# Attention with eleven exponentials on VectorE: other groups, all passes on one engine, and a plan that counts dependent passes

## The chip, the cores and the metric

The kernel runs on one core of a Trainium2 chip. The metric is the device time of the program in microseconds; the median of the runs shown is compared. Engines work in parallel, each on its own queue in the order in which the program issues, and wait for each other by semaphores: TensorE (PE) multiplies, ScalarE (ACT) and VectorE (DVE) work element by element, GpSimd (POOL) does the same more slowly, SyncE (SP) issues DMAs.

## What is computed

Attention for 8 x 8 heads of 512 queries and 512 keys with 64 channels, in float32 at the borders:

```python
q, k, v: (8, 8, 512, 64) float32
scores = einsum('bhqd,bhkd->bhqk', q, k) / sqrt(64)
attn = exp(scores - scores.max(-1)); attn = attn / attn.sum(-1)
out = einsum('bhqk,bhkd->bhqd', attn, v)
```

The kernel leaves the maximum out (the quotient is the same) and takes the sum of a row from a column of ones beside v.

## The kernel before

**Tiling.** The 64 heads are taken as 32 pairs g. A pair's q, k and v come by three DMAs of 256 KB from SyncE's queue (`load`, L440) into buffers that hold seven pairs. Each is cast to float16 by GpSimd (`cast`, L446 and L456; 12 buffers of v, 5 of q with k). TensorE transposes q and k of a pair in eight steps (`transposes`, L480) into one PSUM bank, and VectorE copies them to SBUF (`copy`, L493). For a block of 128 keys by 512 queries one matmul makes the scores, keys on the partitions. Two blocks are a **group**: its scores `st` fill two PSUM banks, and there are three such buffers. Four groups belong to a pair, 129 "groups" in all, the last two being halves.

**Two ways to take the exponential.** Most groups go to ScalarE: one ACTIVATE over 128 x 1024 elements (L527) reads `st` and writes float16 `pt`. The groups in `ON_DVE`, eleven of them, go to VectorE. TensorE first puts a constant into `st` by two more matmuls (L508). VectorE's **raise** (L544) reads `st` from PSUM, scales it, cuts it off below and writes `z` to SBUF, which frees `st`. Three **passes** (L561) from SBUF to SBUF then work out a polynomial on the bits: y from z, y from y, and `pd` from y and z; each needs the one before. `z` and `y` have two buffers each, `pd` four.

The second pass of the last group of `ON_DVE` is an exception (`SHARED = 1`): GpSimd does it in two instructions (`middle`, L574 and L577).

**Values.** A unit of values is four matmuls (L604), blocks of `pt` or `pd` as weights against v with its column of ones, 65 columns out. Seven units share a PSUM bank `o`. When a bank is full, VectorE takes the reciprocal of the sums (L582) and multiplies (L584) into a ring of 56 units in SBUF (together a **norm**), and SyncE stores each head of four units (L593). Transposes and values take turns on the same two PSUM banks. The last head goes its own way: `last_values` (L620) and `finish` (L634, L635).

**What sets the order.** Engines take their instructions in the order in which the program issues them, and that order is made ahead by the class `Plan`. It steps through time by 5 ns with a table of durations (`EXP`, `COPY`, `NORM`, `RAISE`, `PASS` and so on) and decides what each engine does next. `step_pe` prefers scores when a buffer of `st` is free and ScalarE's backlog is short, and else takes transposes or values. `step_dve` takes, of what is ready, a copy that is needed soon, then a raise, then the oldest; passes only fill the time when nothing comes within the margins in `late`. `emit` writes a cast into the order beside a VectorE instruction that reads PSUM. The result is a list of steps that is issued as it stands. The plan's times are for ordering only; on the chip each instruction waits for its semaphores.

A cast can be tied to the VectorE instruction issued last before it (`cast_behind`, L467), by a semaphore, so that it doesn't run while a pass reads SBUF. The plan asks for this when its time is over `CALM`. A pair's v counts as late, and is loaded and cast 6 us later by the plan's due times, when its first group is in `ON_DVE`.

Of the kernel before, what the change touches and what calls it, by code (L numbers as in the profile page):

```python
# [8 lines left out]
FP32 = mybir.dt.float32  # L9
# [8 lines left out]
class Plan:  # L18
# [6 lines left out]
    COPY, NORM, RAISE = (601, 690), (307, 390), (1132, 1215)  # L25
    COPY_1 = (400, 190)
    NORM_COLUMN, PASS_DONE = 67, 80
    PASS, PASSES = 1131, 3
    OFFSET = 216
    FIRST_EXP = 5130  # L30
    STEP = 5
    CALM, KEEN = 14000, 6
    FIRST_UNIT = 4
    ON_DVE = (7, 20, 28, 40, 51, 56, 70, 80, 84, 98, 112)
    SHARED = 1

    LATE_NORM, LATE_COPY, HURRY, SOON, BACKLOG = 1000, 2200, 900, 80, 1200
    SLACK, AHEAD = 0, 2

    CAST, CAST_DONE, TO_POOL = 560, 130, 150  # L40
    MIDDLE, MIDDLE_DONE = (1000, 2250), 250
# [3 lines left out]
    def __init__(self, groups, pairs, first):  # L45
# [26 lines left out]

        late = {grp[0][0] for m, grp in enumerate(groups) if m in self.ON_DVE}
        due = []
# [79 lines left out]
    def for_dve(self, m):  # L154
        return m in self.ON_DVE

# [125 lines left out]
    def step_dve(self, t):  # L282
        if self.uncast and self.uncast[0][1:] == (1, "q"):
            if self.landed.get((1, "q"), 1e9) <= t:
                self.emit(t, None)
                self.dve = t + 240
                self.pool = self.port = t + 330
                self.cast_done[(1, "q")] = t + 400
            return
        now = [x for x in self.ready if x[0] <= t]  # L290
        if now:
            g = self.groups[min(self.m + 1, len(self.groups) - 1)][0][0]
            job = min(now, key=lambda x: (x[1] != "copy" or x[2][0] > g, x[1] != "raise", x[0]))
            self.ready.remove(job)
            _, kind, what = job
            slots = 2 if kind == "raise" else 1
            while slots and not self.casts and self.fits(t, 60 if slots == 1 else 0):
                self.emit(t, self.dve_done if self.dve_done > t - 300 else None)
                slots -= 1
                if slots and self.fits(t, 500):  # L300
                    self.emit(t, self.dve_done if self.dve_done > t - 300 else None)
                    slots -= 1
            self.note(t, kind, *what)
            if kind == "norm":
                more = self.NORM_COLUMN * what[1]
                self.dve = t + self.NORM[0] + more
                self.banks[what[2]] = t + self.NORM[1] + more + self.TO_PE
                for _ in range((what[0] + what[1]) // 4 - what[0] // 4):
                    self.loads.append(("store", self.dve + 100))
            elif kind == "finish":  # L310
                self.dve = t + self.NORM[0] + 2 * self.NORM_COLUMN
            elif kind == "copy":
                held, done = self.COPY if what[0] != 1 else self.COPY_1
                self.dve = t + held
                self.banks[what[1]] = self.tq[what[0]] = t + done + self.TO_PE
            else:
                self.dve = t + self.RAISE[0]
                self.read[what[0]] = t + self.RAISE[1] + self.TO_PE
                self.passes += [(what[0], s, 0) for s in range(self.PASSES)]
            self.dve_done = self.dve  # L320
        elif any(x[2] <= t for x in self.passes):
            m, s, _ = job = next(x for x in self.passes if x[2] <= t)
            end = max(t, self.port) + self.PASS
            late = {"copy": self.LATE_COPY, "norm": self.LATE_NORM, "raise": self.LATE_NORM, "finish": 0}
            if all(x[0] > end - late[x[1]] for x in self.ready):
                self.passes.remove(job)
                self.note(t, "pass", m, s)
                self.dve = self.port = self.dve_done = end
                if s == 0 and m in self.ON_DVE[len(self.ON_DVE) - self.SHARED :]:
                    self.passes.remove((m, 1, 0))  # L330
                    self.passes[self.passes.index((m, 2, 0))] = (m, 2, 1e9)
                    self.casts.append(("middle", m, end + self.TO_POOL))
                    self.note(end, "middle", m)
                if s == self.PASSES - 1:
                    self.exps[m] = end + self.PASS_DONE + self.TO_PE + self.SLACK

# [17 lines left out]
def kernel(  # L354
# [7 lines left out]
    nc = tc.nc  # L362
    B, H, S, D = q.shape
    P = 128
# [25 lines left out]
    opool = ctx.enter_context(tc.tile_pool(name="out", bufs=4))  # L390
# [17 lines left out]
    blocks = {}  # L408
    os = {}
    heads = []  # L410
    raised = {}
    first = {}
    last = {}

    def source(src, g):
        b, h = g // ppb, 2 * (g % ppb)
        return src[b, h : h + 2].rearrange("h (p i) d -> p h i d", i=NI)
# [12 lines left out]
    def load(g, names):  # L430
        if g >= NP:
            return
        for name in names:
            src = {"q": q, "k": k, "v": v}[name]
            t = load_tile(g, name)
            if name == "v" and g in HALVED:
                for h in range(2):
                    nc.sync.dma_start(out=t[:, h], in_=source(src, g)[:, h])
                continue
            nc.sync.dma_start(out=t[:, :, :, :], in_=source(src, g))  # L440
# [22 lines left out]
    def dve(ins):  # L463
        latest[:] = [ins]
        return ins
# [18 lines left out]
    def copy(g, n=0):  # L484
        if g == 1:
            dve(
                nc.vector.tensor_copy(
                    out=tqk[g][:, n], in_=tps[g][:, n].rearrange("p i c -> p (i c)")
                )
            )  # L490
            return
        dve(
            nc.vector.tensor_copy(  # L493
                out=tqk[g][:, :, :], in_=tps.pop(g).rearrange("p n i c -> p n (i c)")
            )
        )
# [74 lines left out]
    def middle(m):  # L571
# [4 lines left out]
        )  # L576
        nc.gpsimd.tensor_tensor(out=y[:, :, :], in0=t[:, :, :], in1=y[:, :, :], op=AluOp.mult)  # L577

    def normalise(u, n):
        o, x = os[u // 7], u % 7  # L580
        rc = opool.tile([P, 7, 1], FP32, tag="rc", name=f"rc_{u}")
        nc.vector.reciprocal(out=rc[:, 0:n], in_=o[:, x : x + n, D : D + 1])  # L582
        dve(
            nc.vector.tensor_tensor(  # L584
                out=ring[:, u % NU : u % NU + n, :],
                in0=o[:, x : x + n, 0:D],
                in1=rc[:, 0:n].broadcast_to([P, n, D]),
                op=AluOp.mult,
            )
        )  # L590
        while heads and heads[0][2] + NI <= u + n:
            g, h, u0 = heads.pop(0)
            nc.sync.dma_start(  # L593
                out=source(out, g)[:, h], in_=ring[:, u0 % NU : u0 % NU + NI, :]
            )
# [48 lines left out]
    def first_loads():  # L644
        tk = load_tile(0, "k")
        tq = load_tile(0, "q")
        for h in range(2):
            nc.scalar.dma_start(out=tk[:, h], in_=source(k, 0)[:, h])
            nc.sync.dma_start(out=tq[:, h], in_=source(q, 0)[:, h])
# [94 lines left out]
    with tc.manual_schedule():  # L744
        plan = Plan(groups, NP, 3)
        steps = plan.run()
        first_loads()
        for g, name in plan.first_loads:
            load(g, name)
        make_identity(nc, ident)  # L750
        nc.vector.memset(lift, LIFT[0])
        for p in (32, 96):
            nc.vector.memset(lift[p : p + 32], LIFT[1])
        for n in range(NV):
            nc.vector.memset(vps[n][:, :, :, D : D + 1], 1.0)
        first_pair()
        do = {
            "transposes": transposes,
            "scores": scores,
            "values": values,  # L760
            "load": load,
            "cast": cast_behind,
            "raise": raise_,
            "copy": lambda g, b: copy(g),
            "pass": pass_,
            "middle": middle,
            "last": last_values,
            "finish": finish,
            "norm": lambda u, n, b: normalise(u, n),
        }  # L770
        for what, *args in steps:
            do[what](*args)
# [30 lines left out]
```

## Time and profile before

| | |
|---|---|
| time, median of 3 runs | 117.99 us (117.93 to 118.18) |
| the profiled execution | 117.88 us, its span 116.1 us |
| granted TensorE clock, mean | 0.992 |
| first exponential starts | 5.11 us |
| last exponential ends | 112.74 us |
| ScalarE's exponentials L527 | 115, busy 104.8 us |
| VectorE's raises L544 and passes L561 | 11 and 32 |
| GpSimd's two instructions for one pass | 1.04 and 2.36 us |

The span is the time from the first to the last instruction of the profiled execution; the rest of its 117.88 us lies around it. Busy rows of one engine can overlap: an instruction's start is recorded before the end of the one ahead of it. So the pitch of an engine is read from start to start or from end to end, not from the durations. An idle time in brackets is the engine's, ahead of the first instruction of the row, with what ended it.

The tail, all engines in order of time (start us, duration us, engine, line):

```profile
111.54 1.21 ACT L527 ACTIVATE pt<-st 128x512 f16<-128x512 f32 x2
112.31 0.79 PE L620 MATMUL o_last<-vp,pt 128*128 128x65 f16 x12 [0.19 <-ACT pt L527]
113.14 0.17 DVE L634 RECIPROCAL rc_last<-o_last 128x2 f32<-128x2 f32 x1
113.34 0.29 DVE L635 TENSOR_TENSOR obl<-o_last,rc_last 128x128 f32<-128x128 f32 x1
113.66 0.35 ACTq L642 DMA_DIRECT2D out_dram<-obl  x1
```

The last values wait for the last exponential, two short VectorE steps follow, and the last store ends the program.

### The profile page before, as it was taken

Reading aid. Unit: us, or ns where it says so; the run is one execution under the profiler, and the core shown is the slowest. Engines: PE = TensorE matmul, PEld = TensorE weight load, DVE = VectorE, ACT = ScalarE, POOL = GpSimd, SP = SyncE. Lnnn points to the kernel's source line nnn. Section 1 sums busy time; section 2 is a strip of 40 time slices with the busy share of each in tenths; the row PEclk is TensorE's granted clock in tenths of the full one; section 3 lists DMA queues with packets and bytes.
Section 4 is the critical chain, followed back from the end, with each engine's and each line's share of the span. In section 5 each row is a group of like instructions: output and inputs, shape, how many; then the busy total and the mean of one; then the engine's idle time right before and its main releaser. Section 6 shows DMA issues by size and latency. Waiting matters only on the chain.

```text
span 116.1 us, 4085 instructions
## 1 busy us (share of the span) xinstructions
PE 104.8 (90%) x1581; PEld 66.9 (58%) x1581; DVE 101.4 (87%) x177; ACT 109.7 (95%) x122; POOL 60.5 (52%) x104
## 2 busy tenths in 40 slices
PE   7979989989999999999799979999989999999980
PEld 2635557546676466646465646467845567576660
DVE  3455997699999999999999999999999999969381
ACT  4599999999999999999999999999999999999980
POOL 2378519954653655555425546954484255596000
PEclk9999999999999999999999999999999999999996
DMA  3999999999999999999999999999999994222354
GB/s 109 286 372 380 384 378 384 388 375 375 344 323 319 307 293 336 311 338 307 352 307 305 321 328 241 296 376 324 329 292 358 366 291 167 93 93 93 101 184 133
DMA packets 35604, 33.83 MB, mean 291 GB/s; under 512 B 2688, under 2 KB 35584, under 8 KB 35584
## 3 DMA queue, kind: packets, MB, share of 16 engines
q1 hardware_dynamic: 35152, 33.24, 87.1%
q10 hardware_dynamic: 432, 0.33, 0.9%
q8 instruction: 12, 0.20, 0.7%
q14 instruction: 8, 0.07, 0.2%
HBM read 25.17 MB, written 8.39 MB: 289 GB/s over the span
## 4 chain that ended last, share of the span: by engine, by line
ACT 31%; DVE 30%; PE 18%; DMA 10%; issue 7%; POOL 1%; SPq 0%; POOLq 0%; ACTq 0%
ACT pt L527 29%; DVE y L561 7%; DVE tqk L493 6%; DMA k<-in_k_dram 6%; DVE z L544 6%; PE st L522 6%; PE o L604 6%; DVE ring L584 5%; DMA v<-in_v_dram 4%; DVE pd L561 4%; PE st_0a L653 3%; ACT pt L703 2%; PE tp L480 2%; POOL qkp L456 1%; DVE rc L582 1%
## 5 line engine op out<-in xcount | busy, mean ns | idle before, releaser
L527 ACT ACTIVATE pt<-st 128x1024 f16<-128x1024 f32 (+1 forms) x115 | 104.8, 1216 | 0.0
L522 PE MATMUL st<-tqk 64*128 64x512 f16 (+1 forms) x250 | 44.6, 380 | 4.3 <-ACT pt L527 3.1
L604 PE MATMUL o<-vp,pt 128*128 128x65 f16 x920 | 43.0, 194 | 1.4 <-DVE tqk L493 0.9
L604 PEld LDWEIGHTS <-pt 128*128 128x128 f16 x920 | 36.3, 98 | 11.0 <-issue 9.7
L446 POOL CAST vp<-v 128x512 f16<-128x512 f32 x32 | 19.6, 616 | 18.6 <-DVE y L561 10.9
L456 POOL CAST qkp<-k 128x512 f16<-128x512 f32 x31 | 19.0, 613 | 14.1 <-PE st L522 4.7
L584 DVE TENSOR_TENSOR ring<-o,rc 128x448 f32<-128x448 f32 (+2 forms) x37 | 22.6, 612 | 1.3
L456 POOL CAST qkp<-q 128x512 f16<-128x512 f32 x30 | 18.4, 613 | 10.1 <-DVE y L561 4.8
L522 PEld LDWEIGHTS <-tqk 64*128 64x128 f16 x250 | 13.1, 93 | 17.6 <-issue 10.1
L493 DVE COPY tqk<-tp 128x1024 f16<-128x1024 f16 x30 | 20.3, 683 | 2.3 <-PE tp L480 2.2
L480 PE MATMUL tp<-ident,qkp 128*128 128x128 f16 x248 | 20.5, 220 | 0.6 <-DVE tqk L493 0.2
L480 PEld LDWEIGHTS <-qkp 128*128 128x128 f16 x248 | 14.2, 97 | 8.8 <-issue 4.8
L561 DVE SCALAR_TENSOR_TENSOR pd<-y,z 128x1024 uint32<-128x1024 f32 x11 | 14.2, 1288 | 0.0
L544 DVE TENSOR_SCALAR z<-st 128x1024 f32<-128x1024 f32 x11 | 13.4, 1217 | 0.9 <-PE st L522 0.9
L561 DVE SCALAR_TENSOR_TENSOR y<-z 128x1024 f32<-128x1024 uint16 x11 | 13.9, 1261 | 0.1
L604 PE MATMUL o<-vp,pd 128*128 128x65 f16 x88 | 13.1, 194 | 0.3 <-DVE pd L561 0.2
L561 DVE SCALAR_TENSOR_TENSOR y<-y 128x1024 f32<-128x1024 f32 x10 | 12.3, 1234 | 0.0
L604 PEld LDWEIGHTS <-pd 128*128 128x128 f16 x88 | 8.6, 98 | 3.2 <-issue 2.4
L582 DVE RECIPROCAL rc<-o 128x7 f32<-128x7 f32 (+2 forms) x37 | 7.3, 196 | 3.3 <-PE o L604 3.2
L508 PE MATMUL st<-const-bfloat16-1.0,lift 64*128 64x512 bf16 x22 | 4.3, 381 | 0.4 <-ACT pt L527 0.4
L653 PE MATMUL st_0a<-const-bfloat16-1.0 128*128 128x512 bf16 (+1 forms) x11 | 3.5, 482 | 0.8 <-PEq L787 0.8
L653 PEld LDWEIGHTS <-const-bfloat16-1.0 128*128 128x128 bf16 x15 | 1.7, 129 | 2.5 <-issue 2.4
(50 smaller groups left out, 25.0 us busy)
## 6 DMA issues: line engine op xcount, KB each, us to landing
out_dram<-ring SPq DMA_DIRECT2D x63, 128.0 KB, 3.8
k<-in_k_dram SPq DMA_DIRECT2D x31, 256.0 KB, 5.1
q<-in_q_dram SPq DMA_DIRECT2D x31, 256.0 KB, 5.0
v<-in_v_dram SPq DMA_DIRECT2D x27, 256.0 KB, 5.2
v<-in_v_dram SPq DMA_DIRECT2D x10, 128.0 KB, 4.1
k<-in_k_dram ACTq DMA_DIRECT2D x2, 128.0 KB, 2.9
q<-in_q_dram SPq DMA_DIRECT2D x2, 128.0 KB, 2.7
out_dram<-obl SPq DMA_DIRECT2D x1, 64.0 KB, 1.6
```

The costliest lines, as they stand in the source:

```text
L446: return nc.gpsimd.tensor_copy(out=vps[g % NV][:, :, :, 0:D], in_=raw[g]["v"][:, :, :, :])
L456: return nc.gpsimd.tensor_copy(out=dst, in_=src[:, :, :, :])
L480: nc.tensor.transpose(tps[g][:, n, i, :], qkp[g][:, n, i, :], ident)
L493: nc.vector.tensor_copy(out=tqk[g][:, :, :], in_=tps.pop(g).rearrange("p n i c -> p n (i c)"))
L522: nc.tensor.matmul(st[:, x, cols], kc, qc[:, cols], start=not on_dve, stop=True)
L527: nc.scalar.activation(out=pt[:, :, cols], in_=st[:, :, cols], func=EXP, scale=scale)
L544: nc.vector.tensor_scalar(out=r["z"][:, :, :], in0=r["st"][:, :, :], scalar1=STEP, scalar2=2.0**17, op0=AluOp.mult, op1=AluOp.max,)
L561: nc.vector.scalar_tensor_tensor(out=r["bits"][:, :, :] if last else r["y"][:, :, :], in0=r["y"][:, :, :] if s else f, scalar=QUARTIC[s], ...
L582: nc.vector.reciprocal(out=rc[:, 0:n], in_=o[:, x : x + n, D : D + 1])
L584: nc.vector.tensor_tensor(out=ring[:, u % NU : u % NU + n, :], in0=o[:, x : x + n, 0:D], in1=rc[:, 0:n].broadcast_to([P, n, D]), op=AluOp. ...
L604: nc.tensor.matmul(os[u // 7][:, u % 7, :], blocks[(g, c, h)][:, y * P : (y + 1) * P], vps[g % NV][:, h, c, :], start=(c == 0), stop=(c == ...
L653: nc.tensor.matmul(dst[:, 0:n], ones[:, 0:P], ones[:, 0:n], start=True, stop=True)
```

## The change

- `ON_DVE` lists eleven other groups: 8, 20, 25, 41, 47, 56, 65, 78, 90, 100, 111 in place of 7, 20, 28, 40, 51, 56, 70, 80, 84, 98, 112. With it other pairs' v count as late, so the loads and casts change their order from the sixth load on.
- `SHARED = ()`: no pass goes to GpSimd.
- The plan lets a pass start only `CHAINED` (117 ns) after the end of the pass or raise it needs, so that other work can come between. Before, all three passes of a group were ready at once.
- `CALM` goes from 14000 to 20000, and the margins and thresholds of the plan change (`LATE_COPY`, `HURRY`, `BACKLOG`, `SLACK`, a new `LATE_MULT`).
- A reciprocal can be issued apart from its multiply (`recip` and `mult`, `invert`), if `APART` is set. It is `False`, and the order that is issued has no such step.

All the rest of the order follows from the plan.

```diff
--- before.py
+++ after.py
@@ -25,17 +25,19 @@
     COPY, NORM, RAISE = (601, 690), (307, 390), (1132, 1215)
     COPY_1 = (400, 190)
     NORM_COLUMN, PASS_DONE = 67, 80
+    RECIP, RECIP_DONE, CHAINED = 80, 230, 117
+    APART, ROOM = False, -200
     PASS, PASSES = 1131, 3
     OFFSET = 216
     FIRST_EXP = 5130
     STEP = 5
-    CALM, KEEN = 14000, 6
+    CALM, KEEN = 20000, 6
     FIRST_UNIT = 4
-    ON_DVE = (7, 20, 28, 40, 51, 56, 70, 80, 84, 98, 112)
-    SHARED = 1
-
-    LATE_NORM, LATE_COPY, HURRY, SOON, BACKLOG = 1000, 2200, 900, 80, 1200
-    SLACK, AHEAD = 0, 2
+    ON_DVE = (8, 20, 25, 41, 47, 56, 65, 78, 90, 100, 111)
+    SHARED = ()
+
+    LATE_NORM, LATE_MULT, LATE_COPY, HURRY, SOON, BACKLOG = 1000, 1600, 1800, 800, 80, 1800
+    SLACK, AHEAD = 100, 2
 
     CAST, CAST_DONE, TO_POOL = 560, 130, 150
     MIDDLE, MIDDLE_DONE = (1000, 2250), 250
@@ -293,6 +295,23 @@
             job = min(now, key=lambda x: (x[1] != "copy" or x[2][0] > g, x[1] != "raise", x[0]))
             self.ready.remove(job)
             _, kind, what = job
+            early = [x for x in now if x is not job and x[1] == "norm"] if self.APART else []
+            apart = kind == "norm" and self.APART and any(x[2] <= t for x in self.passes)
+            apart = apart and self.banks[1 - what[2]] <= t + self.ROOM
+            if kind == "norm" and (early or apart):
+                self.note(t, "recip", *what)
+                kind = "mult"
+                if not early:
+                    self.dve = t + self.RECIP
+                    self.ready.append((t + self.RECIP_DONE, "mult", what))
+                    return
+            for x in early:
+                self.ready.remove(x)
+                self.note(t, "recip", *x[2])
+                t += self.RECIP
+                self.ready.append((t + self.RECIP_DONE - self.RECIP, "mult", x[2]))
+            if early and kind == "mult" and job[1] == "norm":
+                t += self.RECIP_DONE - self.RECIP
             slots = 2 if kind == "raise" else 1
             while slots and not self.casts and self.fits(t, 60 if slots == 1 else 0):
                 self.emit(t, self.dve_done if self.dve_done > t - 300 else None)
@@ -301,8 +320,10 @@
                     self.emit(t, self.dve_done if self.dve_done > t - 300 else None)
                     slots -= 1
             self.note(t, kind, *what)
-            if kind == "norm":
+            if kind in ("norm", "mult"):
                 more = self.NORM_COLUMN * what[1]
+                if kind == "mult":
+                    more -= self.RECIP_DONE
                 self.dve = t + self.NORM[0] + more
                 self.banks[what[2]] = t + self.NORM[1] + more + self.TO_PE
                 for _ in range((what[0] + what[1]) // 4 - what[0] // 4):
@@ -316,21 +337,24 @@
             else:
                 self.dve = t + self.RAISE[0]
                 self.read[what[0]] = t + self.RAISE[1] + self.TO_PE
-                self.passes += [(what[0], s, 0) for s in range(self.PASSES)]
+                self.passes += [(what[0], s, 1e9 if s else self.dve + self.CHAINED) for s in range(self.PASSES)]
             self.dve_done = self.dve
         elif any(x[2] <= t for x in self.passes):
             m, s, _ = job = next(x for x in self.passes if x[2] <= t)
             end = max(t, self.port) + self.PASS
             late = {"copy": self.LATE_COPY, "norm": self.LATE_NORM, "raise": self.LATE_NORM, "finish": 0}
+            late["mult"] = self.LATE_MULT
             if all(x[0] > end - late[x[1]] for x in self.ready):
-                self.passes.remove(job)
                 self.note(t, "pass", m, s)
                 self.dve = self.port = self.dve_done = end
-                if s == 0 and m in self.ON_DVE[len(self.ON_DVE) - self.SHARED :]:
-                    self.passes.remove((m, 1, 0))
-                    self.passes[self.passes.index((m, 2, 0))] = (m, 2, 1e9)
+                after = self.passes.index(job)
+                del self.passes[after]
+                if s == 0 and m in self.SHARED:
+                    self.passes.remove((m, 1, 1e9))
                     self.casts.append(("middle", m, end + self.TO_POOL))
                     self.note(end, "middle", m)
+                elif s < self.PASSES - 1:
+                    self.passes[after] = (m, s + 1, end + self.CHAINED)
                 if s == self.PASSES - 1:
                     self.exps[m] = end + self.PASS_DONE + self.TO_PE + self.SLACK
 
@@ -408,6 +432,7 @@
     blocks = {}
     os = {}
     heads = []
+    rcs = {}
     raised = {}
     first = {}
     last = {}
@@ -576,10 +601,16 @@
         )
         nc.gpsimd.tensor_tensor(out=y[:, :, :], in0=t[:, :, :], in1=y[:, :, :], op=AluOp.mult)
 
+    def invert(u, n):
+        o, x = os[u // 7], u % 7
+        rcs[u] = opool.tile([P, 7, 1], FP32, tag="rc", name=f"rc_{u}")
+        dve(nc.vector.reciprocal(out=rcs[u][:, 0:n], in_=o[:, x : x + n, D : D + 1]))
+
     def normalise(u, n):
         o, x = os[u // 7], u % 7
-        rc = opool.tile([P, 7, 1], FP32, tag="rc", name=f"rc_{u}")
-        nc.vector.reciprocal(out=rc[:, 0:n], in_=o[:, x : x + n, D : D + 1])
+        if u not in rcs:
+            invert(u, n)
+        rc = rcs.pop(u)
         dve(
             nc.vector.tensor_tensor(
                 out=ring[:, u % NU : u % NU + n, :],
@@ -766,7 +797,9 @@
             "middle": middle,
             "last": last_values,
             "finish": finish,
+            "recip": lambda u, n, b: invert(u, n),
             "norm": lambda u, n, b: normalise(u, n),
+            "mult": lambda u, n, b: normalise(u, n),
         }
         for what, *args in steps:
             do[what](*args)
```

## The prediction

> **What bounds the kernel now.** I read the page's busy times first, then the busy time by stretch, then ScalarE's, VectorE's and GpSimd's instructions in order of time. The first two:
>
> ```profile
> span 116.1 us, 4085 instructions
> PE 104.8 (90%) x1581; PEld 66.9 (58%) x1581; DVE 101.4 (87%) x177; ACT 109.7 (95%) x122; POOL 60.5 (52%) x104
> ...
> core 0: us, PE busy (x) PEld busy (x) DVE busy (x) ACT busy (x) POOL busy (x), PEclk, DMA share, GB/s
> 5.00:21.00 16.00, 14.13 (x214) 8.90 (x212) 11.72 (x21) 15.89 (x19) 10.45 (x18) 1.00 1.08 379
> 21.00:41.00 20.00, 18.85 (x267) 11.68 (x265) 19.04 (x28) 20.00 (x23) 11.60 (x21) 1.00 1.03 346
> 41.00:61.00 20.00, 18.64 (x293) 12.03 (x290) 19.76 (x29) 19.96 (x23) 9.57 (x17) 1.00 1.00 319
> 61.00:81.00 20.00, 18.65 (x285) 11.88 (x285) 19.68 (x31) 20.00 (x23) 12.05 (x21) 1.00 0.99 312
> 81.00:101.00 20.00, 19.03 (x314) 12.55 (x313) 19.67 (x29) 20.00 (x23) 10.05 (x17) 1.00 0.85 280
> ```
>
> ScalarE is busy 20.00 of 20.00 us in three stretches; only 41 to 61 has a crack (19.96). VectorE is nearly as full from 21 to 101. Whether ScalarE loses anything shows in the ends of its exponentials (start plus duration; the starts overlap):
>
> ```profile
> 46.44 1.94 ACT L527 ACTIVATE pt<-st 128x1024 f16<-128x1024 f32 x2
> ...
> 47.34 1.95 ACT L527 ACTIVATE pt<-st 128x1024 f16<-128x1024 f32 x2
> ...
> 49.33 1.02 ACT L527 ACTIVATE pt<-st 128x1024 f16<-128x1024 f32 x1
> ...
> 49.33 1.94 ACT L527 ACTIVATE pt<-st 128x1024 f16<-128x1024 f32 x2
> ```
>
> The ends are 48.38, 49.29, 50.35, 51.27: steps of 0.91, 1.06, 0.92. Over the 112 steps between full exponentials, 110 are 0.915 to 0.918, one is 0.929 (46.5 us) and one 1.058 (50.3 us). So ScalarE waits 0.012 + 0.141 = 0.15 us in all, and the time is its work, 0.917 a group, plus the head and tail. The change leaves ScalarE's 115 exponentials, the head and the tail's last steps as they are. **The floor is therefore 117.88 - 0.15 = 117.73** on the profiled execution's own time (span 116.1 and 1.78 around it). The median of the runs, 117.99, is 0.11 above that execution.
>
> VectorE, from which ScalarE's waits come:
>
> ```profile
> 34.94 1.22 DVE L561 SCALAR_TENSOR_TENSOR y<-y 128x1024 f32<-128x1024 f32 x1
> 36.07 0.68 DVE L493 COPY tqk<-tp 128x1024 f16<-128x1024 f16 x1
> 36.67 0.20 DVE L582 RECIPROCAL rc<-o 128x7 f32<-128x7 f32 x1
> 36.90 0.62 DVE L584 TENSOR_TENSOR ring<-o,rc 128x448 f32<-128x448 f32 x1
> 37.44 1.51 DVE L561 SCALAR_TENSOR_TENSOR pd<-y,z 128x1024 uint32<-128x1024 f32 x1
> ...
> 48.28 1.22 DVE L544 TENSOR_SCALAR z<-st 128x1024 f32<-128x1024 f32 x1
> 49.53 1.23 DVE L561 SCALAR_TENSOR_TENSOR y<-z 128x1024 f32<-128x1024 uint16 x1
> ...
> 37.26 0.61 POOL L456 CAST qkp<-q 128x512 f16<-128x512 f32 x1
> 39.01 0.62 POOL L446 CAST vp<-v 128x512 f16<-128x512 f32 x1 [1.14 <-DVE pd L561]
> ```
>
> From start to start a pass or a raise costs 1.13, a copy 0.60, a reciprocal with its multiply 0.77. A pass straight behind its own input starts 1.25 later, not 1.13: 0.12 for the dependence. A pass that meets a cast is stretched: the one at 37.44 takes 1.51, 0.29 too long, while the cast of 37.26 runs to 37.87. Six passes are over 1.30 (1.35, 1.38, 1.51, 1.32, 1.60, 1.55), 1.4 us too much together.
>
> **Part by part.** *The shared group.* Group 112's second pass was two GpSimd instructions, 1.04 + 2.36 us; now all 33 passes are VectorE's. That is +1.13 on VectorE. Passes straight behind their own input fall from four to two in the order of the changed program: -2 x 0.12. Net +0.9 us. It lies in the tail: between 102.6 and 110 VectorE has waits for PE of 0.67, 0.26 and 1.62 us, 2.55 in all, and the last group is now 111. Cost 0; without that cover, 0.9.
>
> The Trainium skill (VectorE: DVE Perf Modes, The DRAIN you can't avoid) says that semaphores between chained VectorE operations cost nothing extra; by it the 0.12 would not exist and the net would be +1.13, still under the cover. The 1.25 beside 1.13 speaks against it here.
>
> *The new places.* VectorE has no idle time to speak of between 21.75 and 102.6, so I weigh its work from one raise to the next against ScalarE's groups between them. Before, 20 to 28: 1 raise, 3 copies, 2 norms, 2 passes = 1.13 + 1.80 + 1.54 + 2.26 = 6.74, against 7 x 0.917 = 6.42: +0.32. All ten so, before: -2.25, +0.32, -0.31, +0.24, -0.69, -0.25, +0.68, -0.42, -0.78, +0.53. After, with the counts of its order: -1.50, -0.03, -0.11, -0.78, +0.53, -0.60, -0.10, -0.03, -0.21, +0.07. The new load is evener. What a surplus does is seen in the trace: measured from raise 20 (21.75) at 0.917 a group, raises 28, 40, 51, 56, 70, 80, 84, 98, 112 start 0.47, 0.61, 0.86, 0.19, -0.03, 0.76, 0.34, -0.05, 0.49 late. ScalarE's two waits fall around the 0.86; 0.76 cost nothing. So I take the 0.15 as gone: -0.15 (bounds -0.15 and 0).
>
> *Around group 20.* In the new order TensorE issues the eight transposes of pair 6 ahead of the scores of 20, and VectorE their copy ahead of raise 20; before, both stood behind. Eight transposes hold PE about 0.55 (0.61 as a row with its drain), and the copy ends some 0.2 after the scores: raise 20 is 0.75 later. First, group 21's scores, next on PE, are later by as much. Before, they ended 0.33 ahead of the end of exponential 19, and waits begin when that lead falls under 0.2 (the 0.012 wait had 0.20). What PE does ahead of them also differs (six units of values of 0.13 where it had more), so the wait is between 0 and 0.23; I take the middle, 0.11. Second, the lateness goes on: 0.75 - 0.03 = 0.72 at raise 25, - 0.11 = 0.61 at raise 41, plus stretched passes: before, 0.59 came together from raise 20 to 51, of which I put 0.45 here: 1.06, which is 0.2 over the 0.86 that cost 0.15, so 0.35; with no stretch, 0. I take 0.15, nearer the low end, as a wait of ScalarE at 21 also takes off lateness. Queued behind a late raise on VectorE are the copy and norms, and for these PE waits, then the scores.
>
> *Casts without a wait.* The border from which a cast is tied to the last VectorE instruction moves from 14 to 20 us. In the new program five casts (v3, k5, q5, v2, v4) wait for their loads alone. Before, casts ran 0.68 apart as loads landed (8.18, 8.85, 9.53 up to 12.26), so these come at about 12.9 to 15.7, where group 8's passes run. The nearest row is the stretched pass, 0.11 to 0.38 each, so 0.3 to 1.15 for three. VectorE's cover is the idle time ahead of raise 20:
>
> ```profile
> 19.10 0.20 DVE L582 RECIPROCAL rc<-o 128x7 f32<-128x7 f32 x1 [0.33 <-PE o L604]
> ...
> 20.19 0.69 DVE L493 COPY tqk<-tp 128x1024 f16<-128x1024 f16 x1 [0.23 <-PE tp L480]
> 21.75 1.22 DVE L544 TENSOR_SCALAR z<-st 128x1024 f32<-128x1024 f32 x1 [0.87 <-PE st L522]
> ```
>
> These are 1.43 us, over 1.15: cost 0, bounds -0.1 (q5 ready sooner, so its transposes) and +1.0 (no cover, PE waits for copies).
>
> The Trainium skill (SBUF — State Buffer, Who interferes with whom) has a rule that speaks against this part: a VectorE operation with two SBUF inputs and a GpSimd operation that reads SBUF exclude each other for a whole instruction. By it each pass could lose a whole cast, 0.61 x 3 = 1.8 us (an estimate), 0.4 over the cover; no pass in the trace loses so much (0.38 at most).
>
> *The rest.* The first loads change places (v1 from the tenth to the sixth) and later ones shift; most loads land microseconds ahead of their casts, and v8, which had 0.1 us, is loaded earlier: 0, bounds -0.1 and +0.1. The split of reciprocal and multiply is switched off (no such step in the order): 0.
>
> Sum: 117.88 - 0.15 + 0.11 + 0.15 = 117.99 for a profiled execution, plus the 0.11 that the median stands above it: **118.10**, 0.09% above 117.99.
>
> **Rivals.** A measurement of this kernel can tell about 0.2%, 0.24 us, so "same" is 117.75 to 118.23.
> *Floor reached:* the even spacing leaves ScalarE without a wait. For it: no surplus over +0.53, and that one behind -0.78. Against: raise 20. 117.73 to 117.85; the time can hardly be lower, as nothing shortens an exponential.
> *Slower, by raise 20's lateness:* VectorE is behind from 22 us and does not recover before raise 47. It decides once lateness plus stretch passes 0.86. At raise 25: 0.72 + 0.3 = 1.02, a wait of 0.26 over the free 0.76; at raise 41 another 0.34; with 0.23 at group 21 that is 0.83 on the floor: 117.73 + 0.83 + 0.11 = 118.67 at most, 118.45 in the middle. Against: the two smaller budgets that follow are negative.
> *Slower, by the untied casts:* passes of group 8 lose over 1.43 us together, the copies of pairs 4 and 5 come late, and PE waits before 21 us: 0.2 to 1.0 us, 118.3 to 119.1. Against: the stretched passes so far lose 0.38.
> *Nothing moves:* the waits only change places, 117.9 to 118.1; it is within the forecast.
>
> **Chances.** The forecast, with the last rival, 0.48 (117.85 to 118.23); floor 0.17, of which 0.07 lies under 117.75; lateness 0.22; casts 0.13. So faster 0.07, same 0.48 + 0.10 = 0.58, slower 0.35. The range 117.75 to 118.65 leaves out 0.06 below and about 0.08 above.
>
> **What would show it.** ScalarE's ends: steps of 0.917 without the 1.058 at 50.3, one longer step at group 21 (22 to 23 us), perhaps one at 25 to 28 and one at 41 to 44. VectorE: 33 passes and two with a start 1.25 behind their input; raise 20 near 22.5 instead of 21.75; stretched passes of group 8 between 13 and 18; the last pass done before 107. GpSimd: no 2.36 row, five casts between 12.9 and 17 with no wait for VectorE. It is wrong if ScalarE's steps sum to over 0.8 us of waits, or if the tail behind the last exponential grows.

## Result, and the profile after

The changed kernel took 118.66 us in the median of 22 runs, the kernel before 118.20 in 22 runs of the same session: a ratio of 1.0043 [1.0027, 1.0059]; the brackets hold its 95% interval. Ratios are formed from the undisturbed executions alone and can differ from the quotient of the printed medians by up to 0.15%. The change makes the kernel slower by 0.43%, about 0.5 us. The profiled execution after took 118.78 us where the one before took 117.88, 0.90 more. First the page of the kernel after: its span, its busy times, and, of its two DMA queues that carry transfers of the kind "instruction", q14 (number of transfers, MB, share of the DMA engines).

```profile
span 117.0 us, 4086 instructions
PE 104.1 (89%) x1581; PEld 66.4 (57%) x1581; DVE 101.6 (87%) x178; ACT 109.9 (94%) x122; POOL 59.9 (51%) x102
...
q14 instruction: 7, 0.06, 0.1%
```

GpSimd has 102 instructions instead of 104, and VectorE one more: the pass that moved. The queue's line will matter further down. Next, the busy time by stretch of the kernel after, with the columns that the prediction showed for before:

```profile
core 0: us, PE busy (x) PEld busy (x) DVE busy (x) ACT busy (x) POOL busy (x), PEclk, DMA share, GB/s
5.00:21.00 16.00, 13.35 (x173) 7.72 (x168) 11.24 (x19) 15.66 (x19) 12.85 (x17) 1.00 1.08 371
21.00:41.00 20.00, 18.87 (x305) 12.47 (x301) 18.72 (x28) 19.97 (x23) 11.52 (x20) 1.00 1.05 353
41.00:61.00 20.00, 18.97 (x290) 11.90 (x290) 19.74 (x31) 19.97 (x23) 11.91 (x21) 1.00 1.00 330
61.00:81.00 20.00, 17.95 (x278) 11.37 (x277) 19.76 (x29) 20.00 (x23) 8.44 (x16) 1.00 0.98 314
81.00:101.00 20.00, 18.74 (x312) 12.51 (x312) 19.63 (x32) 20.00 (x24) 11.12 (x19) 1.00 0.77 255
```

From 61 to 101 us ScalarE is busy without a break. It has little idle time from 21 to 61 us (0.06; rows that overlap hide part of a wait) and 0.23 us more than before in the first stretch. ScalarE's instructions from 39 to 44 us, in order of time, show the whole loss in the middle (start, duration, and so on as before):

```profile
39.23 1.22 ACT L552 ACTIVATE pt<-st 128x1024 f16<-128x1024 f32 x1
40.48 1.02 ACT L552 ACTIVATE pt<-st 128x1024 f16<-128x1024 f32 x1
41.40 1.02 ACT L552 ACTIVATE pt<-st 128x1024 f16<-128x1024 f32 x1
42.44 1.02 ACT L552 ACTIVATE pt<-st 128x1024 f16<-128x1024 f32 x1
```

The ends are 40.45, 41.50, 42.42 and 43.46: steps of 1.05, 0.92, 1.04 where 0.917 is the pitch. That is two waits of 0.13, at groups 42 and 44 around raise 41 (which starts at 40.52), 0.264 in all, against 0.153 before. The other steps are at the pitch. So ScalarE explains 0.11 of the 0.90 us.

The head explains 0.33: the fifth exponential ends at 9.28 instead of 8.95. TensorE's instructions at 5 us, the kernel before and then the kernel after:

```profile
5.02 0.38 PE L696 MATMUL st<-qt,kt 64*128 64x512 f16 x2
5.33 0.40 PE L691 MATMUL tp_qb<-ident,q 128*128 128x128 f16 x4
```

```profile
5.02 0.64 PE L727 MATMUL st<-qt,kt 64*128 64x512 f16 x2
5.59 0.61 PE L722 MATMUL tp_qb<-ident,q 128*128 128x128 f16 x4
```

The same instructions start at the same time and take 0.64 and 0.61 instead of 0.38 and 0.40. The trace's record of the granted clock has full speed from 4.88 us before and from 6.39 us after. This is not the change's doing, as the last section shows.

The rest, 0.46, lies behind everything that the kernel computes. The tail of the kernel after, all engines:

```profile
112.76 0.79 PE L651 MATMUL o_last<-vp,pt 128*128 128x65 f16 x12 [0.19 <-ACT pt L552]
113.58 0.17 DVE L665 RECIPROCAL rc_last<-o_last 128x2 f32<-128x2 f32 x1
113.79 0.29 DVE L666 TENSOR_TENSOR obl<-o_last,rc_last 128x128 f32<-128x128 f32 x1
114.11 0.35 ACTq L673 DMA_DIRECT2D out_dram<-obl  x1
```

The last store is issued at 114.11 instead of 113.66, 0.45 later, which is the head and ScalarE's waits together. But the span ends 0.93 later, so from the store's issue to the end it takes 0.48 us more. The last store is not quite the end of the program: it takes 1.6 us to land, and then GpSimd runs the last instructions. The other engines wait for it: their last semaphore instructions come at 116.93 to 116.94 after the change, right behind GpSimd's at 116.89. GpSimd's instructions from 115 us of the kernel before and of the kernel after (count: shortest, median and longest duration in ns, start of the first and of the last):

```profile
L798 POOLq EVENT_SEMAPHORE  x4: 17/17/17, 115.4 to 116.0; - x4
L798 POOLq DRAIN  x2: 34/56/78, 115.6 to 115.8; - x2
L798 POOLq EVENT_SEMAPHORE_RANGE_CLEAR  x1: 94/94/94, 115.7 to 115.7; - x1
```

```profile
L831 POOLq EVENT_SEMAPHORE  x4: 17/17/17, 115.9 to 116.9; - x4
L831 POOLq DRAIN  x2: 78/130/183, 116.0 to 116.6; - x2
L831 POOLq EVENT_SEMAPHORE_RANGE_CLEAR  x1: 94/94/94, 116.2 to 116.2; - x1
```

These seven are the same in both: two semaphore instructions, a drain, the range clear, the second drain, two more semaphore instructions. Before, they run from 115.4 to 116.0 and the second drain starts 0.1 after the range clear. After, it starts 0.4 after it and takes 183 ns instead of 34: a hole of about 0.45 us in an end that the change doesn't touch.

### The profile page after: what moved, and what is told of

The parts are those of the page before. It is cut to its first block, busy times and chain, and to the rows that moved or that the text cites. A ratio compares the mean times of both kernels' runs of the same rounds, so it can differ in the third digit from the quotient of the medians.

```text
span 117.0 us, 4086 instructions
## 1 busy us (share of the span) xinstructions
PE 104.1 (89%) x1581; PEld 66.4 (57%) x1581; DVE 101.6 (87%) x178; ACT 109.9 (94%) x122; POOL 59.9 (51%) x102
## 4 chain that ended last, share of the span: by engine, by line
ACT 36%; PE 26%; DVE 22%; issue 7%; DMA 5%; POOL 2%; ACTq 0%; POOLq 0%; SPq 0%
ACT pt L552 35%; PE o L635 9%; PE st L547 8%; DVE y L586 5%; DMA q<-in_q_dram 5%; DVE ring L615 5%; DVE pd L586 4%; DVE tqk L518 3%; PE st_0a L684 3%; PE tp L505 3%; DVE z L569 2%; DVE rc L607 1%; POOL qkp L481 1%; ACT pt L734 1%; PE st L727 1%
## 5 line engine op out<-in xcount | busy, mean ns | idle before, releaser
L547 PE MATMUL st<-tqk 64*128 64x512 f16 (+1 forms) x250 | 43.8, 379 | 6.8 <-ACT pt L552 5.8
L481 POOL CAST qkp<-k 128x512 f16<-128x512 f32 x31 | 20.9, 673 | 23.2 <-DVE y L586 4.9
L471 POOL CAST vp<-v 128x512 f16<-128x512 f32 x32 | 20.4, 647 | 9.9 <-DVE pd L586 4.8
L505 PE MATMUL tp<-ident,qkp 128*128 128x128 f16 x248 | 19.6, 219 | 0.7 <-POOL qkp L481 0.4
L586 DVE SCALAR_TENSOR_TENSOR y<-y 128x1024 f32<-128x1024 f32 x11 | 13.8, 1262 | 0.0
```

The costliest lines, as they stand in the source:

```text
L471: return nc.gpsimd.tensor_copy(out=vps[g % NV][:, :, :, 0:D], in_=raw[g]["v"][:, :, :, :])
L481: return nc.gpsimd.tensor_copy(out=dst, in_=src[:, :, :, :])
L505: nc.tensor.transpose(tps[g][:, n, i, :], qkp[g][:, n, i, :], ident)
L547: nc.tensor.matmul(st[:, x, cols], kc, qc[:, cols], start=not on_dve, stop=True)
L586: nc.vector.scalar_tensor_tensor(out=r["bits"][:, :, :] if last else r["y"][:, :, :], in0=r["y"][:, :, :] if s else f, scalar=QUARTIC[s], ...
```

## Experiments

Two theories had to be told apart. *The order:* the new places and the untied casts disturb VectorE, and ScalarE waits; the runs then differ by what ScalarE loses. *The end:* the new order is as good as the old one, and the hole at the end of GpSimd's program costs the time. For the second there was a hint in the number of GpSimd's records in the trace (instructions, waits and semaphore instructions together): 203 before, 199 after. If GpSimd took its instructions in blocks, with a border behind every 128 records and some offset, then with 199 records a border could fall among the last seven, and with 203 ahead of them, where GpSimd waits eight to ten microseconds for the end anyway. This can be tested: GpSimd instructions with nothing to do move the border.

**Four memsets behind the identity in the head, in the changed kernel**

```diff
         make_identity(nc, ident)
+        spare = cpool.tile([P, 64], FP32, name="spare")
+        for n in range(4):
+            nc.gpsimd.memset(spare[:, n : n + 1], 0.0)
```

> The changed kernel with four tiny GpSimd memsets of a spare tile added in the head, where GpSimd waits for the first load; every other engine's order is as it was. Theory A (the end of GpSimd's program): the changed kernel loses 0.45 us between GpSimd's last range-clear and its last drain (116.24 to 116.76, against 115.77 to 115.84 in the kernel before) because its stream is four instructions shorter (199 records against 203) and a block border of its instruction fetch falls there; with four more the gap goes, the end takes 0.07 again, and the ratio falls from 1.0043 to about 1.0005. Theory B (ScalarE's waits and the late start of TensorE's full clock make the loss): the end of GpSimd's program changes nothing in the median, and the ratio stays at 1.003 to 1.006.

Measured: 117.96 us, 0.9981 [0.9957, 1.0005]. GpSimd's end in this kernel:

```profile
L834 POOLq EVENT_SEMAPHORE  x4: 17/17/17, 115.7 to 116.3; - x4
L834 POOLq DRAIN  x2: 34/56/78, 115.9 to 116.1; - x2
L834 POOLq EVENT_SEMAPHORE_RANGE_CLEAR  x1: 96/96/96, 116.0 to 116.0; - x1
```

With 203 records the hole is gone: 34 ns for the second drain, 0.1 behind the range clear, as before the change. Adding four instructions made the kernel faster, and the whole loss is gone with the hole.

**The same in the kernel before, as a control.** The diff is the same.

> The kernel before with the four memsets in the head, 207 records. Theory A: the border stays hidden behind GpSimd's wait for the end, ratio 0.999 to 1.001. Theory C: the memsets help here as well, ratio 0.994 to 0.997.

Measured: 118.11 us, 0.9988 [0.9946, 1.0030], 207 records, no hole. The memsets by themselves gain nothing that can be told.

**All passes on VectorE, nothing else changed**

```diff
-    SHARED = 1
+    SHARED = 0
```

> The kernel before with SHARED = 0: the last group's second pass on VectorE, all else as it was. GpSimd's stream loses the two instructions of the middle pass. Theory A: one to three fewer records put the border inside GpSimd's last steps, +0.3 to +0.45 us, ratio 1.003 to 1.004, though ScalarE has no new wait. Theory B: the added pass is covered by 2.5 us of idle VectorE time in the tail, so the ratio is 0.999 to 1.001.

Measured: 118.78 us, 1.0066 [1.0040, 1.0093], more than either theory had. This kernel has 202 records, and its hole is at another place. GpSimd's end:

```profile
L798 POOLq EVENT_SEMAPHORE  x4: 17/17/17, 116.0 to 117.0; - x4
L798 POOLq DRAIN  x2: 34/86/138, 116.5 to 116.8; - x2
```

The first semaphore instruction is at 116.0, the drain that follows the second one only at 116.5: the hole, 0.36, lies between the first two semaphore instructions and not behind the range clear. In both kernels that is behind GpSimd's record 196: with 202 records it is the first of the last seven, with 199 the fourth. With 203 it is the last one ahead of them.

**The same with four memsets**

> The same with four GpSimd memsets in the head. Theory A: the gap at the end of GpSimd's program is gone, ratio 0.999 to 1.001. Theory B: as without them.

Measured: 118.20 us, 1.0003 [0.9982, 1.0023], 206 records and no hole. Taking all passes onto VectorE costs nothing that shows.

**124 memsets behind the last cast, in the kernel before.** If the border comes back every 128 records, 327 records are as bad as 199.

```diff
+        spare = cpool.tile([P, 128], FP32, name="spare")
+        for n in range(124):
+            nc.gpsimd.memset(spare[:, n : n + 1], 0.0)
```

> The kernel before with 124 GpSimd memsets of a spare tile behind its last cast, where GpSimd waits some 7.7 us for the end; nothing else moves. Theory A with a border every 128 records: so far the border stood behind record 196 in all four kernels that showed a gap or could have; 203 + 124 = 327 records put the next border (196 + 128 = 324) between the range-clear and the last drain, so the kernel before should lose the 0.45 us of the changed kernel: ratio 1.003 to 1.005. If the border stands elsewhere or doesn't repeat every 128: 0.999 to 1.001, as the 124 memsets at 0.035 us each (4.3 us) fit into the wait. Theory C (memsets in the head help for another reason, and the end has nothing to do with it): 0.999 to 1.001.

Measured: 118.55 us, 1.0027 [0.9998, 1.0055]. GpSimd's end:

```profile
L801 POOLq EVENT_SEMAPHORE  x4: 17/17/17, 115.6 to 116.7; - x4
L801 POOLq DRAIN  x2: 77/132/188, 115.8 to 116.3; - x2
L801 POOLq EVENT_SEMAPHORE_RANGE_CLEAR  x1: 96/96/96, 115.9 to 115.9; - x1
```

The hole is back: the last drain ends 0.51 us behind the end of the range clear, where it was 0.07 in the kernel before. That is behind record 196 + 128 = 324, in a kernel that has the old order throughout. So it belongs to the number of GpSimd's records and not to the order. The ratio is 0.32 us over 118.2, by its interval -0.02 to 0.65; the hole's 0.45 lies within, though no loss at all just does too. The median is a little under the 1.003 to 1.005 that was expected.

**Repeat of the changed kernel, without and with the memsets**

> The changed kernel as it is, a second profile and more runs. Theory A: ratio 1.003 to 1.006, the gap between range-clear and drain again (0.5 us). The start of TensorE's full clock, 6.39 us in its first profile against 4.88, lies anywhere between 4.8 and 6.8 if it is a matter of the execution; at 6.3 to 6.5 again if it is the kernel's. ScalarE's waits 0 to 0.3 us.

> The changed kernel with the four memsets once more, to narrow the interval (0.9957 to 1.0005 in the first set). If the new order is worth something by itself, the ratio stays under 1, 0.997 to 0.999, with ScalarE's waits under 0.15 us; if the first set was lucky, 0.999 to 1.001.

Measured: 118.74 us, 1.0045 [1.0014, 1.0076], with the hole, and 117.97 us, 0.9976 [0.9946, 1.0006], without it. ScalarE's waits were 0.56 us in the one profile (0.19 of it in the head) and 0.07 in the other; in the first pair of profiles 0.26 and 0. So they vary by some tenths between executions (all counted behind the fifth exponential). Full clock began at 3.73 us in the repeat, earlier than the expectation allowed; the last section comes back to that.

**The new places alone, in the kernel before**

```diff
-    ON_DVE = (7, 20, 28, 40, 51, 56, 70, 80, 84, 98, 112)
+    ON_DVE = (8, 20, 25, 41, 47, 56, 65, 78, 90, 100, 111)
```

> The kernel before with the new eleven groups alone (GpSimd keeps the middle pass of group 111, the casts keep their border of 14 us, and the plan does not count the delay). Theory A: what the median does follows from the end of GpSimd's program: no gap there and a ratio of 0.999 to 1.002, or the gap and 1.004. Theory B: the new places bring ScalarE waits of 0.3 us or more by themselves, ratio over 1.003, seen as steps over 0.917 us between the ends of exponentials.

Measured: 119.85 us, 1.0149 [1.0114, 1.0184], 202 records and the hole. From the last exponential's end to the end of the span it takes 4.30 us, 0.98 more than before, of which the hole is 0.36. The time is above what the hole alone was to give, and ScalarE's waits are there too, 0.8 us.

> The new places under the old plan, with four GpSimd memsets in the head (206 records, so the border is hidden). Theory A takes off the gap of 0.36 us that the run without them showed between GpSimd's two end waits: ratio 1.010 to 1.013 in place of 1.0149. What is left are ScalarE's waits (0.8 us in that profile, the longest 0.37 us at 29 us and 0.23 at 46) and a later end of the last values (0.6 us). If the places were as good under either plan, it would be 0.997 to 0.999.

Measured with four memsets: 119.37 us, 1.0087 [1.0055, 1.0119], no hole; less is left than the expectation had. The tail is still 3.94 us, where the padded kernel before has 3.31. The chain that ended last goes over TensorE's scores and values there, without a pause from 107.3 to 112.7 us, and not over the last exponential; so values were still being worked off. The rest is ScalarE's. Its instructions around 29 us in this kernel:

```profile
26.45 2.12 ACT L527 ACTIVATE pt<-st 128x1024 f16<-128x1024 f32 x2
28.86 2.85 ACT L527 ACTIVATE pt<-st 128x1024 f16<-128x1024 f32 x3 [0.29 <-PE st L522]
```

The bracket is a wait for scores, one of three (at 12.5, 28.6 and 45.5 us) that make 1.2 us by the ends. Under the old plan the new places are bad.

**The old places in the changed kernel** (with six memsets, so that the hole is out)

```diff
-    ON_DVE = (8, 20, 25, 41, 47, 56, 65, 78, 90, 100, 111)
+    ON_DVE = (7, 20, 28, 40, 51, 56, 70, 80, 84, 98, 112)
```

> The changed kernel with the eleven old groups put back, the rest of the new plan kept, and six memsets (204 records, border hidden). If the gain of the padded change (0.998) comes from the plan's new count and margins, this is 0.997 to 1.000; if it needs the new places, ScalarE waits over 0.3 us and the ratio is 1.001 to 1.006.

Measured: 119.45 us, 1.0088 [1.0058, 1.0117], 203 records, no hole; seven waits of ScalarE, 1.6 us together. That is more than either case of the expectation. Under the new plan the old places are as bad as the new ones are under the old plan.

**The changed kernel with a plan that doesn't count the delay** (with eight memsets)

```diff
-    RECIP, RECIP_DONE, CHAINED = 80, 230, 117
+    RECIP, RECIP_DONE, CHAINED = 80, 230, 0
```

> The changed kernel with CHAINED = 0 in place of 117, so that the plan lets a pass follow its input at once, and eight memsets (204 records). On the chip a pass behind its input still starts 0.12 us later. If counting the delay is what makes the new plan hold, VectorE falls behind it: the budget from raise 41 to 47 is +1.55 us in this order, ScalarE waits 0.3 us or more there and the ratio is 1.002 to 1.010. If the count hardly matters, 0.997 to 1.000.

Measured: 119.81 us, 1.0134 [1.0095, 1.0174], above the expected range; 205 records, no hole. ScalarE from 43 to 49 us:

```profile
42.98 1.96 ACT L552 ACTIVATE pt<-st 128x1024 f16<-128x1024 f32 x2
45.37 1.94 ACT L552 ACTIVATE pt<-st 128x1024 f16<-128x1024 f32 x2 [0.43 <-PE st L547]
47.63 1.94 ACT L552 ACTIVATE pt<-st 128x1024 f16<-128x1024 f32 x2 [0.32 <-PE st L547]
```

Two waits for scores ahead of and behind raise 47. In this order VectorE has 1.55 us more work from raise 41 to raise 47 than ScalarE's groups between them give it; in the changed kernel it had 0.78 less. ScalarE's waits are 1.8 us in all. The 0.12 us on the chip hardly enter into this: in this order only one pass starts straight behind its own input (at 17.11 us), and two do in the changed kernel. So the run shows that another order loses, and not what the delay costs.

**The changed kernel with casts tied from 14 us on, as before** (with six memsets)

```diff
-    CALM, KEEN = 20000, 6
+    CALM, KEEN = 14000, 6
```

> The changed kernel with CALM = 14000 as before, and six memsets (207 records). The casts of 14 to 20 us wait for VectorE again; the passes of group 8 are no longer stretched (1.38 and 1.51 us in the changed kernel) and the casts there no longer take 1.5 to 1.6 us. I had put this part at 0: ratio 0.997 to 1.000, with the stretched rows gone. If the untied casts cost something, it is under the padded change, 0.995 to 0.997; if they are needed, over 1.001.

Measured: 117.87 us, 0.9980 [0.9951, 1.0009]. The casts wait again, and the passes are not stretched. GpSimd of this kernel, then GpSimd of the changed kernel, in the same stretch:

```profile
14.85 0.62 POOL L471 CAST vp<-v 128x512 f16<-128x512 f32 x1 [1.90 <-DVE y L586]
...
18.61 0.62 POOL L481 CAST qkp<-q 128x512 f16<-128x512 f32 x1 [2.54 <-DVE pd L586]
```

```profile
13.76 1.48 POOL L481 CAST qkp<-k 128x512 f16<-128x512 f32 x1
...
15.75 2.16 POOL L471 CAST vp<-v 128x512 f16<-128x512 f32 x2
17.85 1.60 POOL L481 CAST qkp<-k 128x512 f16<-128x512 f32 x1
```

Tied, a cast takes 0.62 and starts late; untied, it starts at once and takes up to 1.60. The time is the same, so it makes no difference that shows here where the border `CALM` stands.

## Why the prediction was wrong: the end of the program

**The step that failed** is a clause in the floor: "The change leaves ScalarE's 115 exponentials, the head and the tail's last steps as they are." The instructions of the tail are the same, but their time is not. The change makes GpSimd's program four records shorter, and that moved a border into its last seven instructions. The forecast was 0.11 over the median before; measured were 0.46 to 0.52, of which the hole is 0.45 in the profile. Without the hole the changed kernel ran at 0.9981, 0.9976 and (with `CALM` back at 14000) 0.9980 of before. Each interval just includes 1. The padded kernel before ran at 0.9988, so against that the order itself is worth some 0.1%, and against the one without padding some 0.2%. The 0.15 us between forecast and floor would be 0.13%; it isn't shown that they were gained.

What is shown: the hole comes and goes with the number of GpSimd's records, in both orders; it lies behind record 196 or 324 wherever it appears; with four to eight instructions that do nothing it is gone, with 124 it comes back. What is inferred is that it is the loading of a block of instructions. The queues of the kind "instruction" speak for it in part. Their lines of the page of the kernel before:

```profile
q8 instruction: 12, 0.20, 0.7%
q14 instruction: 8, 0.07, 0.2%
```

The transfers on q14 are of 8192 bytes, and 128 records in each would be 64 bytes for one; those on q8 are of 16384. In the five profiles with the hole the last DMA transfer of all is one of q14; in the nine without it, none is. In the changed kernel it comes at 117.29 us, behind the end of the span, and so the page counts 7 there and not 8. But in all five this transfer begins 1.1 us behind the record ahead of the hole, when the hole has been over for 0.7 us. So it is not what GpSimd waits for; at most the crossing of the border sets it off. What fills the hole stays open, and no run tells a block of instructions from a block of the trace's own records.

That the border comes every 128 records has support in the middle of the program too: behind record 68, which is 196 - 128, ten of the 14 profiles have a gap of 0.37 to 0.43 us on GpSimd, and behind no other record do more than five.

Why GpSimd doesn't get past the border in the ten microseconds in which it waits for the end stays open. So does a part of the size: four pairs of the same kernel without and with the padding differ by 0.62 to 0.69% in their ratios, 0.73 to 0.82 us (0.53 to 0.77 by the medians), and the hole in the profiles is 0.36 to 0.45.

**What held, point by point.**

*All passes on VectorE: cost 0, covered by the tail.* Right: 1.0003 with the hole out. The last pass in the changed kernel:

```profile
105.52 1.22 DVE L586 SCALAR_TENSOR_TENSOR pd<-y,z 128x1024 uint32<-128x1024 f32 x1
```

It is done at 106.74, before the 107 that was named.

*Raise 20 late.* Right in mechanism. It starts at 22.69 (about 22.5 was forecast); 0.94 after the 21.75 of before, 0.33 of which is the head. Raises 25 and 41 start at 26.50 and 40.52. At 0.917 for each of ScalarE's 4 and 15 groups between, that adds 3.81 - 3.67 = 0.14 and 14.02 - 13.76 = 0.27, so raise 41 is 0.61 + 0.14 + 0.27 = 1.02 behind; the prediction had 1.06 with its stretch.

*ScalarE's waits: 0.11 at group 21 and 0.15 later.* The sum is 0.26, and 0.264 was measured, but not there: nothing at group 21, whose scores ended 0.24 us ahead of the end of exponential 19 (0.33 before), and all of it around raise 41. That the total agrees is partly luck, as other executions of the same order had 0 and 0.07 (padded) and 0.56 (unpadded).

*Untied casts: cost 0, with bounds to +1.0.* Right. VectorE's passes of group 8 and its raise 20 in the changed kernel:

```profile
13.55 1.22 DVE L586 SCALAR_TENSOR_TENSOR y<-z 128x1024 f32<-128x1024 uint16 x1
...
16.05 1.38 DVE L586 SCALAR_TENSOR_TENSOR y<-y 128x1024 f32<-128x1024 f32 x1
17.47 1.51 DVE L586 SCALAR_TENSOR_TENSOR pd<-y,z 128x1024 uint32<-128x1024 f32 x1
...
22.69 1.21 DVE L569 TENSOR_SCALAR z<-st 128x1024 f32<-128x1024 f32 x1
```

Two passes are stretched, by 0.16 and 0.29, within the 0.11 to 0.38 of the prediction. The loss falls on the other side: the casts beside them take 1.48 and 1.60 instead of 0.61. The Trainium skill (SBUF — State Buffer, Who interferes with whom) has the two engines exclude each other; here GpSimd pays for it, up to 1 us a cast, and a pass 0.3 at most.

*The plan's budgets.* The prediction read "the new load is evener" as a property of the places. The runs show that places and plan go together: new places under the old plan 1.0087, old places under the new plan 1.0088, the new places under the new plan without its 117 ns 1.0134, all with the hole out. The table of surpluses is no sufficient gauge either: the order of the old places under the new plan has no surplus over +0.53, and yet ScalarE waits seven times.

*The 0.12 us of a dependent pass.* It is on record as a delay of 1.25 beside 1.13. The Trainium skill (VectorE: DVE Perf Modes, The DRAIN you can't avoid) has no extra cost for semaphores in a chain. The rows of the changed kernel have the delay once more: its pass at 79.00 us starts 1.25 after its input, while those at 62.12 and 65.76, each behind a pass of another group, start 1.13 after it. What it is worth to count the delay in the plan isn't shown: the run without the 117 ns lost 1.3% in an order that has the delay only once, and the plan of the kernel before doesn't count it either.

*What would make it wrong* was named as waits of over 0.8 us in all, or a tail that grows. The tail grew: from the last exponential's end to the end of the span 3.80 us instead of 3.32.

The lowest medians are those of the changed kernel with the memsets: 117.96 and 117.97 us, or 117.87 with `CALM` at 14000, beside 118.18 to 118.23 for the kernel before.

## What to carry to other kernels

When a change moves the time by tenths of a microsecond, first lay the last microseconds of both traces side by side, every engine's semaphore instructions too: an engine whose program got some instructions shorter or longer can lose 0.4 us at the very end, and a few instructions that do nothing, placed early, show whether that is so. Judge a new order only with such an accident taken out; here it turned a change worth between nothing and 0.2% into a loss of 0.43%. And places that were chosen under one plan are to be judged under that plan: each half of this change by itself cost about 0.9%.

## What the runs showed of the hardware

*TensorE's full clock starts at different times.* Over 14 profiles it is granted from 3.73 to 6.77 us on, whatever the kernel: 6.39 and 3.73 in two executions of the same changed kernel. The first matmul starts at 0.77 us in all of them. From the start of the first exponential to the end of the fifth it takes 3.84 us in the eight profiles where full clock begins by 5.34, 4.01 where it begins at 5.76, and 4.14 to 4.23 in the five where it begins from 6.11 on. So a late start costs up to 0.39 us. The first exponential itself starts between 4.82 and 5.34, for reasons that weren't traced, and the fifth ends between 8.67 and 9.49. The heads of the two executions of the changed kernel differ by 0.61 us (9.28 and 8.67), and a difference of profiles has to be cleaned of that before it is explained. The Trainium skill (TensorE: Matmul & The Clock Gate, Part 1: The HAM clock gate) has the transition vary by 500 ns to either side; the spread here is 3.0 us.

*A border in an engine's instructions can be visible.* It lay behind records 196 and 324 of GpSimd, with a gap behind record 68 too, which fits one every 128, and cost 0.36 to 0.45 us where nothing hid it. The Trainium skill (Runtime: NRT & Kernel Launch, Instruction fetch mechanics) has blocks of 256 instructions, whose crossing is mostly hidden. If the hole is such a crossing, as inferred above, these runs show 128 on GpSimd instead, and a crossing that was hidden in nine of 14 profiles and exposed at the end in five.
